# Hybrid attention block in split float32: the order of work in the gated stage and in front of the output projection

## Chip, cores and metric

One NeuronCore of a Trainium2 chip runs the whole kernel as one program. The metric is the device time of one execution in microseconds (us), lower is better. In the profile PE is TensorE's matmul, PEld its weight load, DVE VectorE, ACT ScalarE, POOL GpSimd, and SP SyncE, which here only issues DMAs.

## The reference

One decoder layer on x of 1024 tokens by 1024 channels, all in float32. What matters here is its end. `o_a` and `o_b` are the outputs of two attention mixers (512 channels each), `z_a`, `z_b`, `m_a`, `m_b` are parts of the input projection, and `gate` is the third part of a conditioning vector:

```
mod = c @ w_ada + b_ada                      # shift, scale, gate
y_a = (merge_heads(o_a) * silu(z_a)) @ w_o_nsa
y_b = (merge_heads(o_b) * silu(z_b)) @ w_o_swa
y = (sigmoid(m_a) * y_a + sigmoid(m_b) * y_b) @ w_out
x = x + gate[:, None, :] * rms_norm(y, g_post)
```

## The kernel before

Every float32 operand of a matmul is held as a high part (a copy rounded to the format of TensorE's fast float32) and a low part (operand minus high part), and every product is made of three matmuls: high by high, high by low, low by high. A matmul has 128 output rows and 512 columns. Splitting a weight tile is a cast (the high part) and a subtraction on GpSimd (the low part).

The first stages (conditioning, norm, projections, attention) are not touched. Near the end of attention, blocks of the input projection still run as filler behind a pace set by `hold`; it is cleared at L892. Then come two stages.

**The gated stage** (L896 to L982). `oh`, `ol` are the high and low parts of the eight head tiles, loaded from DRAM as `t1` tiles (named `od` in the code) and split: cast on ScalarE L909, subtraction on VectorE L910. Tiles 4 to 7 belong to side B, 0 to 3 to side A. The first two merge gates are made by projections (L918); the other fourteen are read back from DRAM into `t2` tiles (four buffers), and ScalarE applies the sigmoid (L916). `gated` (L929) then makes one block of 128 output rows: it loads one weight tile `w_o`, splits it (`split_half`: cast L151 on VectorE, subtraction L157 on GpSimd), and makes two halves of 512 columns, 12 matmuls each (L937 to L939). A loop over the eight blocks of side B writes the product with the gate to `ym` (L949, VectorE). A loop over the eight blocks of side A multiplies by the gate (L970, VectorE), adds to `ym` (L971, GpSimd), and splits the sum into `ymh` (L980, ScalarE) and `yml` (L981, VectorE). Behind each block of side A, `w_out_block` loads a row block of the last weight matrix in two halves and splits it: cast L962 on VectorE, subtraction L963 on GpSimd. These go to the places of the normalised input `hh`, `hl`, which the two projected gates read last. All raw weight tiles, `w_o` and `w_out`, share three buffers named `wraw`.

**The output projection** (L984 to L1033). The gate part of the conditioning is formed first: the eight row blocks of `w_adaT` in sixteen half-width loads into `t1` tiles, each reduced on VectorE against a broadcast of c (L992), then two products of `ones` with a diagonal tile `dg`, which lies in a `t2` buffer (L1001 on VectorE, L1004 on TensorE), then copies to `ggb` (L1005). For each of eight row tiles, two halves of 24 matmuls (L1017 to L1019) are followed by the sum of squares (L1021), scaling, adding x and the store.

The tile framework orders the instructions of each engine by the program order, by its own estimate of when operands are ready, and by the buffers. Each engine, and SyncE's queue of DMAs, then runs its list strictly in order.

## Time and profile before

| | us |
|---|---|
| median of three runs (940.97 to 942.63) | 942.55 |
| the profiled execution | 939.97 |
| its span | 938.1 |
| TensorE busy in the span | 913.6 |
| matmuls of the gated stage end (last one's start, rounded) | 833.9 |
| last matmul of the program starts | 931.15 |

The span runs from the first to the last instruction of the profiled execution, whose own time is 1.87 us more. A busy TensorE is not TensorE at its peak: matmuls are pipelined, and a row's duration (0.39) is longer than the distance to the next row (0.23).

### The profile page before, as it was taken

Reading aid. Unit: us, or ns where it says so; the run is one execution under the profiler, and the core shown is the slowest. Engines: PE = TensorE matmul, PEld = TensorE weight load, DVE = VectorE, ACT = ScalarE, POOL = GpSimd, SP = SyncE. Lnnn points to the kernel's source line nnn. Section 1 sums busy time; section 2 is a strip of 40 time slices with the busy share of each in tenths; the row PEclk is TensorE's granted clock in tenths of the full one; section 3 lists DMA queues with packets and bytes.
Section 4 is the critical chain, followed back from the end, with each engine's and each line's share of the span. In section 5 each row is a group of like instructions: output and inputs, shape, how many; then the busy total and the mean of one; then the engine's idle time right before and its main releaser. Section 6 shows DMA issues by size and latency. Waiting matters only on the chain.

```text
span 938.1 us, 14375 instructions
## 1 busy us (share of the span) xinstructions
PE 913.6 (97%) x4584; PEld 762.0 (81%) x4584; DVE 568.9 (61%) x1557; ACT 486.7 (52%) x1116; POOL 380.5 (41%) x438
## 2 busy tenths in 40 slices
PE   9979999999999999999999999999999999979997
PEld 8869888888888878868878888887887888858885
DVE  5847563376677776684676755565664379872322
ACT  5566632266776776584666765665554421342111
POOL 0001212256575874453533764543351226871000
PEclk9989999999999999999999999999999999989999
DMA  8960452323232321212101222111111679621232
GB/s 309 313 216 33 162 165 86 122 79 102 81 106 82 125 60 39 80 35 68 59 32 35 80 68 80 55 48 57 58 46 56 218 234 303 194 89 45 90 107 84
DMA packets 65166, 100.84 MB, mean 107 GB/s; under 512 B 7617, under 2 KB 24385, under 8 KB 65090
## 3 DMA queue, kind: packets, MB, share of 16 engines
q1 hardware_dynamic: 64082, 98.73, 32.4%
q10 hardware_dynamic: 1008, 1.19, 0.4%
q8 instruction: 36, 0.59, 0.2%
q14 instruction: 40, 0.33, 0.1%
HBM read 79.97 MB, written 19.92 MB: 106 GB/s over the span
## 4 chain that ended last, share of the span: by engine, by line
PE 49%; POOL 2%; DVE 2%; DMA 2%; issue 1%; ACT 1%; DVEq 0%; POOLq 0%; SPq 0%; ACTq 0%
PE b_pj L177 6%; PE b_pt L778 6%; PE b_pj L182 5%; PE b_pj L183 5%; PE b_pv L789 3%; PE b_s L725 3%; PE b_pv L786 3%; PE b_s L728 3%; DMA wraw<-in_w_out 1%; PE b_s L1018 1%; PE b_s L1017 1%; PE b_s L1019 1%; POOL ym L971 1%; POOL wol L963 1%; PE b_pj L1017 1%
## 5 line engine op out<-in xcount | busy, mean ns | idle before, releaser
L157 POOL TENSOR_TENSOR wl<-wraw,wh 128x512 fp32r<-128x512 f32 x102 | 134.1, 1315 | 248.3 <-DVE wh L151 145.8
L177 PE MATMUL b_pj<-hh,wh 128*128 128x512 f32 x528 | 210.2, 398 | 0.0
L183 PE MATMUL b_pj<-hh,wl 128*128 128x512 f32 x528 | 208.2, 394 | 0.0
L182 PE MATMUL b_pj<-hl,wh 128*128 128x512 f32 x528 | 207.7, 393 | 0.0
L785 DVE TENSOR_TENSOR pl<-b_pt,ph 128x512 fp32r<-128x512 f32 x178 | 120.7, 687 | 35.6 <-ACT ph L784 34.7
L784 ACT CAST ph<-b_pt 128x512 fp32r<-128x512 f32 x178 | 101.9, 584 | 64.5 <-PE b_pt L778 57.0
L183 PEld LDWEIGHTS b_pj<-hh,wl 128*128 128x128 f32 x528 | 99.3, 188 | 18.9
L177 PEld LDWEIGHTS b_pj<-hh,wh 128*128 128x128 f32 x528 | 99.4, 188 | 17.9
L182 PEld LDWEIGHTS b_pj<-hl,wh 128*128 128x128 f32 x528 | 99.4, 188 | 17.5
L725 PE MATMUL b_s<-kh,q 128*128 128x256 f32 (+6 forms) x264 | 86.6, 334 | 1.4 <-DVE rr L753 0.8
L749 ACT ACTIVATE ps<-ps,mins 128x256 f32<-128x256 f32 (+7 forms) x96 | 65.0, 679 | 38.4 <-DVE mins L735 36.7
L761 POOL TENSOR_SCALAR ps<-ps,rr,gates 128x128 f32<-128x128 f32 (+7 forms) x64 | 52.9, 832 | 78.8 <-DVE rr L753 68.8
L728 PE MATMUL b_s<-kl,q 128*128 128x256 f32 (+6 forms) x264 | 84.0, 323 | 0.0
L749 ACT ACTIVATE pw<-pw,mins 128x256 f32<-128x256 f32 (+4 forms) x96 | 60.6, 632 | 31.5 <-DVE mins L735 29.4
L789 PE MATMUL b_pv<-pl,V 128*128 128x512 f32 x162 | 69.9, 431 | 1.6 <-DVE pl L785 1.4
L786 PE MATMUL b_pv<-ph,V 128*128 128x512 f32 x162 | 68.0, 420 | 0.3 <-ACT ph L784 0.2
L761 POOL TENSOR_SCALAR pw<-pw,rr,gates 128x640 f32<-128x640 f32 (+4 forms) x64 | 47.4, 744 | 50.6 <-DVE rr L753 44.4
L154 ACT CAST wh<-wraw 128x512 fp32r<-128x512 f32 x74 | 45.5, 617 | 36.9 <-PE b_pj L182 35.2
L725 PEld LDWEIGHTS b_s<-kh,q 128*128 128x128 f32 x264 | 49.8, 189 | 10.0 <-DVE mins L735 1.9
L800 POOL TENSOR_TENSOR ot<-ot,zt 64x512 f32<-64x512 f32 x32 | 41.2, 1287 | 34.9 <-DVE ot L799 28.6
L728 PEld LDWEIGHTS b_s<-kl,q 128*128 128x128 f32 x264 | 49.8, 189 | 6.1
L778 PE MATMUL b_pt<-ident,ps 128*128 128x128 f32 x344 | 52.4, 273 | 0.0
(296 smaller groups left out, 1883.8 us busy)
## 6 DMA issues: line engine op xcount, KB each, us to landing
wraw<-in_w_blk SPq DMA_DIRECT2D x90, 256.0 KB, 2.8
wa<-in_w_adaT SPq DMA_DIRECT2D x16, 512.0 KB, 4.9
w1raw<-in_w SPq DMA_DIRECT2D x16, 256.0 KB, 3.4
od<-ot SPq DMA_DIRECT2D x64, 64.0 KB, 2.1
sp_MA<-sp SPq DMA_DIRECT2D x16, 256.0 KB, 2.0
wraw<-in_w_o SPq DMA_DIRECT2D x16, 256.0 KB, 3.8
t<-od SPq DMA_DIRECT2D x16, 256.0 KB, 3.4
xr<-in_x SPq DMA_DIRECT2D x16, 256.0 KB, 4.0
```

The source lines that it names most:

```text
L157: chain("wl", nc.gpsimd.tensor_tensor(wl, raw, wh.bitcast(F32), ALU.subtract))
L177: ins = nc.tensor.matmul(t, lhsT=wh, rhs=hh[kc][half], start=(kc == 0), stop=False)
L182: nc.tensor.matmul(t, lhsT=wh, rhs=hl[kc][half], start=False, stop=False)
L183: nc.tensor.matmul(t, lhsT=wl, rhs=hh[kc][half], start=False, stop=(kc == KC - 1))
L725: ins = nc.tensor.matmul(sp[:, :n_in], lhsT=q, rhs=rh, start=True, stop=False)
L728: nc.tensor.matmul(sp[:, :n_in], lhsT=q, rhs=rl, start=False, stop=True)
L749: nc.scalar.activation(rows[r][:, :off], rows[r][:, :off], AF.Exp, scale=-1.0, bias=mins[:, n - 1, r : r + 1], accum_out=sums[:, r : r + 1])
L761: nc.gpsimd.tensor_scalar(rows[r][:, :off], rows[r][:, :off], rr[:, r : r + 1], gate, ALU.mult, ALU.mult)
L778: ins = nc.tensor.transpose(t[:kw, r * P : r * P + P], rows[r][:, off : off + kw], ident)
L784: nc.scalar.copy(ph[:kw], t[:kw])
L785: nc.vector.tensor_tensor(pl[:kw], t[:kw], ph[:kw].bitcast(F32), ALU.subtract)
L789: nc.tensor.matmul(pv, lhsT=v, rhs=pl[:kw], start=False, stop=(last and n == len(todo) - 1))
```

## The change

Four edits, all behind the attention stage. (1) `ended` is set where `hold` is cleared; from then on `split_half` casts weights on ScalarE, not on VectorE, for the two projected gates and all of `w_o`. The cast of `w_out` moves to ScalarE too. (2) `w_out_block(m)` is called behind each block of side B, ahead of side A; head tiles 0 to 3 are loaded inside that loop, one behind every second block. (3) The sum of the sides is made on VectorE. (4) The gate part of the conditioning loads eight full-width tiles, into places that the gated stage leaves (`ym7`, `oh1`, `ol1`, ..., with c in `ym6`), and its two products stand behind the products of the first two row tiles, which are issued two ahead of their evaluation.

```
-        if low is None and hold[0] is None:
+        if low is None and hold[0] is None and not ended:
             ins = nc.vector.tensor_copy(wh, raw)
             after(ins, last["dve"])
         else:
...
     hold[0] = None
+    ended.append(True)
...
-        for k in (4, 5, 6, 7, 0, 1, 2, 3):
+        def heads_out(k):
             for half in range(2):
...
+        for k in range(4, 8):
+            heads_out(k)
...
-        for m in range(8):
-            ym[m] = op.tile([P, S], F32, name=f"ym{m}", tag=f"ym{m}")
-            gated(m, "B", 1, lambda sl, ty, sg: nc.vector.tensor_tensor(ym[m][:, sl], ty, sg, ALU.mult))
...
-                nc.vector.tensor_copy(a[n], raw)
+                nc.scalar.copy(a[n], raw)
                 nc.gpsimd.tensor_tensor(b[n], raw, a[n].bitcast(F32), ALU.subtract)
...
         for m in range(8):
+            ym[m] = op.tile([P, S], F32, name=f"ym{m}", tag=f"ym{m}")
+            gated(m, "B", 1, lambda sl, ty, sg: nc.vector.tensor_tensor(ym[m][:, sl], ty, sg, ALU.mult))
+            if m % 2:
+                heads_out(m // 2)
+            w_out_block(m)
+        for m in range(8):
             def emit(sl, ty, sg):
                 nc.vector.tensor_tensor(sg, ty, sg, ALU.mult)
-                nc.gpsimd.tensor_tensor(ym[m][:, sl], ym[m][:, sl], sg, ALU.add)
+                nc.vector.tensor_tensor(ym[m][:, sl], ym[m][:, sl], sg, ALU.add)
             gated(m, "A", 0, emit)
...
-            w_out_block(m)
...
-        cbs = [tmp("xr", 3), tmp("xr", 3)]
...
+        cb2 = op.tile([P, D], F32, name="cb2", tag="ym6")
+        nc.sync.dma_start(cb2, io["c"].partition_broadcast(P))
+        for k, place in enumerate(("ym7", "oh1", "ol1", "oh2", "ol2", "oh3", "ol3", "oh1")):
             blk = 16 + k
+            wa = op.tile([P, D], F32, name="wa", tag=place)
+            nc.sync.dma_start(wa, io["w_adaT"][blk * P : (blk + 1) * P, :])
+            nc.vector.tensor_tensor_reduce(
+                out=wa, in0=wa, in1=cb2, scale=1.0, scalar=smalls[:, 8 + blk : 9 + blk],
+                op0=ALU.mult, op1=ALU.add, accum_out=mod[:, blk : blk + 1])
...
+        ahead = [out_products(0), out_products(1)]
+        gate_rows()
+        for i in range(NT):
+            out_rows(i, ahead.pop(0))
+            if i + 2 < NT:
+                ahead.append(out_products(i + 2))
```

`out_products(i)` holds the 48 matmuls of a row tile, `out_rows(i, ts)` what follows them, and `gate_rows` the diagonal tiles, the two products with `ones` and the copies to `ggb`; their bodies are the lines that stood in the loop before.

TensorE's order at the end of the gated stage, before (`oh3`, `ol3` are a head tile's parts; L1004 is a product with `ones`, L1017 to L1019 are products of the first row tile):

```order
L939 MATMUL b_pv_9218<-oh3_8251,wl_9197 128x512
L1004 MATMUL b_pt_9308<-t2_9309,ones_75 128x512
L1017 MATMUL b_pj_9322<-woh0_8824,ymh0_8816 128x512
L1018 MATMUL b_pj_9322<-wol0_8825,ymh0_8816 128x512
L1019 MATMUL b_pj_9322<-woh0_8824,yml0_8817 128x512
```

and in the changed kernel (line numbers shifted; L944 is the last gated matmul, L1011 the product with `ones`):

```order
L944 MATMUL b_pv_9230<-oh3_8251,wl_9209 128x512
L1020 MATMUL b_pt_9282<-woh0_8463,ymh0_8912 128x512
L1021 MATMUL b_pt_9282<-wol0_8464,ymh0_8912 128x512
...
L1022 MATMUL b_s_9357<-woh7_8866,yml7_9249 128x512
L1011 MATMUL b_pt_9382<-t2_9383,ones_75 128x512
L1011 MATMUL b_pj_9387<-t2_9388,ones_75 128x512
L1020 MATMUL b_s_9413<-woh0_8463,ymh0_8912 128x512
```

The products with `ones` moved from directly behind the gated stage to behind 96 products; the first product that reads `yml7` stands 26 matmuls behind the gated stage.

VectorE's order at the end of side A in the changed kernel (L978 the product with the gate, L979 the sum of the sides, L989 the low part, ISA the reductions of the conditioning):

```order
L978 TENSOR_TENSOR t2_9243<-b_pv_9230,t2_9243 128x512
L989 TENSOR_TENSOR yml7_9249<-ym7_8809,ymh7_9248 128x512
L979 TENSOR_TENSOR ym7_8809<-ym7_8809,t2_9243 128x512
L997 ISA wa_9262,mod_83<-wa_9262,cb2_9254,smalls_79 128x1024
L997 ISA mod_83 128x1
L989 TENSOR_TENSOR yml7_9249<-ym7_8809,ymh7_9248 128x512
L997 ISA wa_9259,mod_83<-wa_9259,cb2_9254,smalls_79 128x1024
```

The sums joined VectorE's list between the gate products and the low parts, and all eight reductions now stand behind them, one of them ahead of the last low part.

SyncE's DMAs at the start of side B, before (`in_w_o` weights of a gated block, `od` head tiles, `in_w_out` the last matrix):

```order
L908 DMA t1_8300<-od0_118 128x512
L908 DMA t1_8304<-od1_119 128x512
L908 DMA t1_8308<-od1_119 128x512
L908 DMA t1_8312<-od2_120 128x512
L908 DMA t1_8316<-od2_120 128x512
L908 DMA t1_8320<-od3_121 128x512
L959 DMA wraw_8822<-in_w_out 128x512
L908 DMA t1_8324<-od3_121 128x512
L991 DMA t1_9258<-in_w_adaT 128x512
```

and in the changed kernel (L910 head tiles, L961 the last matrix, L145 weights of a gated block):

```order
L910 DMA t1_8292<-od7_125 128x512
L961 DMA wraw_8575<-in_w_out 128x512
L910 DMA t1_8508<-od0_118 128x512
L145 DMA wraw_8582<-in_w_o 128x512
L910 DMA t1_8512<-od0_118 128x512
L961 DMA wraw_8630<-in_w_out 128x512
L910 DMA t1_8622<-od1_119 128x512
L961 DMA wraw_8636<-in_w_out 128x512
L910 DMA t1_8626<-od1_119 128x512
L145 DMA wraw_8643<-in_w_o 128x512
```

Between two loads for gated blocks now stand two loads of the last matrix and three half head tiles, where before the head tiles stood in a row; the conditioning's loads are gone from here. The `in_w_o` load first shown is the tenth that takes a `wraw` buffer from the first gated block's on, for block 3 of side B; block 0 of side A has the twenty-fifth.

## Rows read from the trace of the kernel before

**Rows 1.** The first part of the profile's page: busy time of each engine, its share of the span and its number of instructions.

```profile
PE 913.6 (97%) x4584; PEld 762.0 (81%) x4584; DVE 568.9 (61%) x1557; ACT 486.7 (52%) x1116; POOL 380.5 (41%) x438
```

**Rows 2.** Busy time of each engine in six stretches (us from the span's start): stage of side B, stage of side A, the gap, the time right behind it, the output projection, the tail. Behind the engines stand the granted TensorE clock as a share of 2.4 GHz, the mean busy share of the DMA engines, and GB/s.

```profile
747.10:790.80 43.70, 43.70 (x194) 36.19 (x193) 34.58 (x63) 10.69 (x18) 18.66 (x13) 1.00 0.82 264
790.80:834.20 43.40, 43.40 (x193) 35.69 (x191) 36.98 (x47) 15.02 (x25) 36.58 (x25) 1.00 0.57 184
834.20:840.20 6.00, 0.15 (x2) 0.04 (x1) 3.30 (x6) 3.52 (x6) 2.97 (x2) 0.83 0.30 94
840.20:846.10 5.90, 5.90 (x12) 3.69 (x13) 3.60 (x6) 1.19 (x3) 3.90 (x3) 0.59 0.00 0
846.10:931.40 85.30, 85.30 (x377) 70.38 (x375) 23.40 (x46) 11.96 (x34) 4.49 (x8) 1.00 0.26 84
931.40:938.10 6.70, 0.14 (x1) 0.00 (x0) 2.22 (x4) 0.69 (x2) 0.55 (x1) 0.68 0.21 79
```

**Rows 3.** TensorE's instructions in order of time around the end of the gated stage, and its last one: start, duration (a matmul's end is modelled and overlaps the next), line, operation; in brackets the idle time before it and what ended that.

```profile
833.93 0.39 PE L939 MATMUL b_pv<-oh,wl 128*128 128x512 f32 x1
...
840.17 2.07 PE L1004 MATMUL b_pt<-t,ones 128*128 128x512 f32 x2 [5.84 <-DVE t L1001]
...
846.12 0.39 PE L1019 MATMUL b_pj<-woh,yml 128*128 128x512 f32 x1
...
849.77 0.39 PE L1017 MATMUL b_s<-woh,ymh 128*128 128x512 f32 x1
...
931.15 0.39 PE L1019 MATMUL b_s<-woh,yml 128*128 128x512 f32 x1
```

**Rows 4.** Who waited for whom around the gap (834 to 850 us): the waits of the compute engines, us in total, times, longest.

```profile
PE b_pt L1004 <- DVE t L1001: 5.8, 1, 5.8
...
DVE t L1001 <- POOL ym L971: 2.3, 2, 1.2
```

**Rows 5.** The same for the DMA queue that SyncE issues, over the gated stage (747 to 850 us).

```profile
SPq L915 <- POOL ym L971: 20.6, 12, 3.0
...
SPq L959 <- POOL wol L963: 7.8, 9, 1.3
...
SPq L144 <- POOL wl L157: 5.0, 5, 1.6
```

**Rows 6.** VectorE, GpSimd and ScalarE behind the end of the gated matmuls, in order of time (one row of each engine).

```profile
844.27 0.69 DVE L970 TENSOR_TENSOR t<-b_pv,t 128x512 f32<-128x512 f32 x1
...
843.84 1.65 POOL L971 TENSOR_TENSOR ym<-ym,t 128x512 f32<-128x512 f32 x1 [1.41 <-DVE t L970]
...
846.77 0.62 ACT L980 CAST ymh<-ym 128x512 fp32r<-128x512 f32 x1
```

**Rows 7.** Groups of instructions by line in the gated stage (747.1 to 834.2 us): busy us, mean ns of one, then the idle time before them and its releasers.

```profile
L963 POOL TENSOR_TENSOR wol<-wraw,woh 128x512 fp32r<-128x512 f32 x16 | 23.4, 1468 | 12.0 <-DVE woh L962 12.0
...
L971 POOL TENSOR_TENSOR ym<-ym,t 128x512 f32<-128x512 f32 x11 | 16.8, 1538 | 1.2 <-DVE t L970 1.2
...
L157 POOL TENSOR_TENSOR wl<-wraw,wh 128x512 fp32r<-128x512 f32 x11 | 15.5, 1409 | 18.4 <-DVE wh L151 14.4 <-DMA wraw<-in_w_out 2.9 <-DVE amod L996 1.0
...
L962 DVE CAST woh<-wraw 128x512 fp32r<-128x512 f32 x16 | 14.6, 916 | 2.3 <-DMA wraw<-in_w_out 2.3
...
L992 DVE CUSTOM_DVE_ANT_0 t<-t,xr,mod 128x512 f32<-128x512 f32 x8 | 9.6, 1201 | 0.9 <-DMA t<-in_w_adaT 0.8
...
L992 DVE CUSTOM_DVE_ANT_0 t<-t,xr,smalls 128x512 f32<-128x512 f32 x8 | 6.8, 846 | 1.5 <-DMA t<-in_w_adaT 1.5
...
L909 ACT CAST oh<-t 128x512 fp32r<-128x512 f32 x10 | 6.2, 622 | 9.8 <-DMA t<-od 9.7
...
L151 DVE CAST wh<-wraw 128x512 fp32r<-128x512 f32 x11 | 6.2, 564 | 2.2 <-DMA wraw<-in_w_o 1.6 <-PE b_s L939 0.6
```

**Rows 8.** Single lines: the low part of the merged rows on VectorE, and the reduction of the conditioning in the first stage at full width (duration ns min/median/max, first and last start).

```profile
L981 DVE TENSOR_TENSOR yml<-ym,ymh x16: 676/1114/1780, 806.4 to 847.4; 128x512 fp32r<-128x512 f32 x16
...
L265 DVE CUSTOM_DVE_ANT_0 wa<-wa,cb,smalls x16: 1278/1280/1284, 13.0 to 47.5; 128x1024 f32<-128x1024 f32 x16
```

**Rows 9.** The loads that share the three raw weight buffers, from the first load of the last matrix to its last (L959 that matrix, L144 the head-side weights): issues with first and last start, then the time to landing.

```profile
L959 SPq DMA_DIRECT2D wraw<-in_w_out x16: 327/328/398, 759.2 to 815.4; - x16
...
DMA to landing us min/median/max: 2.7/3.7/5.0
...
L144 SPq DMA_DIRECT2D wraw<-in_w_o x7: 328/328/383, 766.0 to 810.8; - x7
...
DMA to landing us min/median/max: 2.6/4.1/4.8
```

**Rows 10.** The first stage, where conditioning weights are loaded in pieces of 512 KB while nothing else is large: the stretch of 10 to 50 us (columns as in rows 2), and the time to landing of these loads.

```profile
10.00:50.00 40.00, 39.98 (x224) 35.89 (x223) 34.25 (x67) 21.55 (x40) 0.00 (x0) 1.00 0.89 307
...
DMA to landing us min/median/max: 3.6/4.7/9.5
```

**Rows 11.** The end of attention, around 720 us: a weight cast on VectorE, two rows of ScalarE, and TensorE's next wait.

```profile
720.23 0.42 DVE L151 CAST wh<-wraw 128x512 fp32r<-128x512 f32 x1
...
719.93 0.59 ACT L816 COPY sp<-b_pj 128x512 f32<-128x512 f32 x1 [0.34 <-PE b_pj L183]
...
720.83 0.59 ACT L784 CAST ph<-b_pt 128x512 fp32r<-128x512 f32 x1 [0.31 <-PE b_pt L778]
...
722.19 0.50 PE L789 MATMUL b_pv<-pl,V 128*128 128x512 f32 x1 [0.23 <-DVE pl L785]
```

More of the change, by code (lines that the diff above doesn't have):

```diff
@@ L93, in hybrid_kernel @@
     hold = [None]
+    ended = []
     done = [0.0]
@@ L981, in hybrid_kernel @@
                 nc.vector.tensor_tensor(yml[m][:, sl], ym[m][:, sl], ymh[m][:, sl].bitcast(F32), ALU.subtract)
-            w_out_block(m)
-        cbs = [tmp("xr", 3), tmp("xr", 3)]
-        for n in range(2):
-            nc.sync.dma_start(cbs[n], io["c"][n * HS : n * HS + HS].partition_broadcast(P))
-        for k in range(KC):
-            blk = 16 + k
-            for n in range(2):
-                wa = tmp("t1", 3)
-                nc.sync.dma_start(wa, io["w_adaT"][blk * P : (blk + 1) * P, n * HS : n * HS + HS])
-                nc.vector.tensor_tensor_reduce(
-                    out=wa, in0=wa, in1=cbs[n], scale=1.0,
-                    scalar=mod[:, blk : blk + 1] if n else smalls[:, 8 + blk : 9 + blk],
-                    op0=ALU.mult, op1=ALU.add, accum_out=mod[:, blk : blk + 1])
+        cb2 = op.tile([P, D], F32, name="cb2", tag="ym6")
@@ L996, in hybrid_kernel @@
         nc.vector.tensor_tensor(amod, mod[:, 16:24], g_post, ALU.mult)
         ggb = op.tile([P, D], F32, name="ggb")
-        for n in range(2):
-            t = anybank()
-            dg = tmp("t2", 4)
-            nc.vector.tensor_tensor(
-                dg.rearrange("p (k t) -> p k t", k=4), ident.unsqueeze(1).broadcast_to([P, 4, P]),
-                amod[:, 4 * n : 4 * n + 4].unsqueeze(2).broadcast_to([P, 4, P]), ALU.mult)
-            nc.tensor.matmul(t, lhsT=ones, rhs=dg, start=True, stop=True)
-            nc.scalar.copy(ggb[:, n * HS : n * HS + HS], t)
@@ L1006, in hybrid_kernel, with gate_rows @@
-        for i in range(NT):
+        def gate_rows():
+            for n in range(2):
+                t = anybank()
+                dg = tmp("t2", 4)
+                nc.vector.tensor_tensor(
+                    dg.rearrange("p (k t) -> p k t", k=4), ident.unsqueeze(1).broadcast_to([P, 4, P]),
+                    amod[:, 4 * n : 4 * n + 4].unsqueeze(2).broadcast_to([P, 4, P]), ALU.mult)
+                nc.tensor.matmul(t, lhsT=ones, rhs=dg, start=True, stop=True)
+                nc.scalar.copy(ggb[:, n * HS : n * HS + HS], t)
@@ L1007, in hybrid_kernel, with out_products @@
+        def out_products(i):
             sl = slice(i * P, i * P + P)
-            xr = tmp("xr", 3)
-            xs = [xr, tmp("xr", 3)]
-            ss = sm.tile([P, 2], F32, name="ss", tag="ss", bufs=2)
-            yg = []
+            ts = []
             for n in range(2):
-                ns = slice(n * HS, n * HS + HS)
-                nc.sync.dma_start(xs[n], io["x"][sl, ns])
                 t = anybank()
@@ L1019, in hybrid_kernel, with out_rows @@
                     nc.tensor.matmul(t, lhsT=yml[k][:, sl], rhs=woh[k][n], start=False, stop=(k == 7))
+                ts.append(t)
+            return ts
+        def out_rows(i, ts):
+            sl = slice(i * P, i * P + P)
+            xs, yg = [], []
+            ss = sm.tile([P, 2], F32, name="ss", tag="ss", bufs=2)
+            for n, t in enumerate(ts):
+                ns = slice(n * HS, n * HS + HS)
+                xs.append(tmp("xr", 3))
+                nc.sync.dma_start(xs[n], io["x"][sl, ns])
                 jk = tmp("t2", 4)
@@ L1028, in hybrid_kernel @@
             nc.gpsimd.tensor_tensor(rs, rs, neg1, ALU.pow)
-            nc.vector.tensor_tensor(yg[1], t, ggb[:, HS:], ALU.mult)
+            nc.vector.tensor_tensor(yg[1], ts[1], ggb[:, HS:], ALU.mult)
             for n in range(2):
```

## The prediction

> **What bounds the kernel now.** I read the page first: TensorE is busy 97% of the span [rows 1], so only its idle or slow time can be won. The table by stretches says where that is [rows 2]: in both sides of the gated stage TensorE is full at a granted clock of 1.00, in the output projection again; between them lie 6.0 us without work and 5.9 us at a mean clock of 0.59, that is mostly at the lower of its two levels (1.2 of 2.4 GHz), behind that idle time. TensorE's own rows give the size [rows 3]: the last gated matmul starts at 833.93, the next instruction comes 5.84 us late and is the product with `ones` for the conditioning, and full pace (0.227 us per matmul) is back at 846.12.
>
> The waits name the cause: TensorE waits for VectorE's diagonal tile, which waits for a sum of the sides on GpSimd [rows 4], since that sum frees the `t2` buffer. The second thing to see is that this is not the only late work. VectorE forms the last gate product at 844.27, GpSimd's last sum starts at 843.84, and a cast of `ymh` still starts at 846.77 [rows 6]: the chain behind the matmuls is some 10 us late. It is late because GpSimd is busy 36.58 of 43.40 us in side A [rows 2], with eleven sums and the splits of both weights [rows 7], and because the loads of the gates wait 20.6 us for the sums [rows 5]. Taking away only the product with `ones` would put the wait on `yml7`.
>
> **The gap, the main term.** From 834.16 (833.93 plus one distance of 0.227) to 931.38 are 97.22 us. The work in it is 384 products (8 row tiles, 2 halves, 24 each) and two products with `ones`. Between 849.77 and 931.15 lie 359 distances [rows 3], so one is 81.38 / 359 = 0.2267 us; 384 of them are 87.05. A product with `ones` is two float32 rows: at the low clock the pair took 2.07 [rows 3], at the full clock I take half of that less a little latency, 0.87; two are 1.74. So 88.8 us are needed and 97.22 - 88.8 = 8.4 us are to be had, if nothing is late next and the clock stays at 1.00.
>
> **Is anything late next?** First the chain to `yml7`. Its last gate product can start when the stage ends; the sum of that half belongs to later row tiles. For the first half, a low part follows on VectorE at 0.68 each, the shortest of its line [rows 8], so it is ready 1.5 us behind the stage; the order has 26 matmuls first, 5.9 us. Cover 4.4 us. In side A VectorE now has 48 such instructions (16 gate products, 16 sums, 16 low parts), 48 x 0.68 = 32.6 of 43.4 us, since the casts and, in side B, the reductions are gone from it (16.4 us of L992, 14.6 of L962, 6.2 of L151 [rows 7]). GpSimd loses its sums (1.54 us each [rows 7]) and gains nothing.
>
> A low part took up to 1.78 us, with a median of 1.11, against 0.68 at best [rows 8], beside a GpSimd that hardly paused. The Trainium skill, SBUF — State Buffer, section on who interferes with whom, says that a VectorE instruction with two SBUF inputs and a GpSimd instruction that reads SBUF lock each other out for a whole instruction; that speaks against the sums on VectorE, which have two such inputs. By that rule the eight weight splits left on GpSimd in side A, 1.41 us each, add at most 11.3 us to the 32.6, 43.9 against 43.4: half a microsecond, inside the cover. By the rows' median for the 32 instructions with two inputs the load would be 46.6, 3.2 us too much, inside the cover too.
>
> Second the conditioning. Its eight loads of 512 KB and the broadcast of c, 4.72 MB, can be issued from some 833 us, when the last side A half leaves `oh1`. In the first stage such loads ran at 307 GB/s [rows 10]: 15.4 us. Then the last reduction, 1.28 [rows 8], and a diagonal tile, 0.7: ready at about 852. A slower bound: the first stage's sixteen reductions came one in 2.16 us (13.0 to 47.5 [rows 8]) with other loads between; 833 + 4.7 to the first landing [rows 10] + 8 x 2.16 + 2 gives 857. TensorE needs it behind 96 products, at 834.2 + 21.8 = 856.0. I take no wait, and 1 to 2 us as the far end, on the loads' own rate, as nothing else moves much then.
>
> **Side B, the price.** What was a dense stage gets 16 loads of the last matrix, their casts and their splits. ScalarE: 25.7 us busy in both sides [rows 2] plus 36 casts of 0.62, as the cast L909 takes [rows 7], make 48 of 87.1. GpSimd in side B: 24 splits of 1.47 make 35 of 43.7. Both fit. The tight place is the three `wraw` buffers. From the tenth load (issued at about 749, by the time of the same head tiles now) to the twenty-fifth, which block 0 of side A needs, are 15 loads. That block starts at 747.1 + 8 x 24 x 0.2267 = 790.6; with 4.1 us landing [rows 9], a cast of 0.62, a split of 1.29 and 0.4 of signals its load must be issued by 784.2. So a load may take 35.2 / 15 = 2.35 us. Before, 23 loads went from 759.2 to 815.4 [rows 9], 2.55 each, which would make TensorE wait 3 us. A turn of a buffer by its parts (4.1 landing, 0.62, 1.29) is 6.0 us, 2.0 per load. I take the parts: the old pace was not the buffers' own, since the queue stood 20.6 us for sums that leave GpSimd and 12.8 us for splits [rows 5], and a cast of `w_out` took 0.92 us beside GpSimd on VectorE [rows 7]. Cost nothing, far end 3 us.
>
> **The end of attention.** Six weight casts now stand on ScalarE between the casts of the probabilities. Around 720 us a cast of 0.6 comes beside a copy at 719.93 and pushes the cast at 720.83; TensorE then already waits 0.23 us [rows 11]. It costs between 0 and 1.2 us (two such places); I take 0.3, since elsewhere ScalarE pauses and VectorE is relieved.
>
> **Sum.** 8.4 - 0.3 = 8.1 us. The profiled execution goes from 939.97 to 931.9, its span from 938.1 to 930.0. It is 2.6 us below the median of the three runs; the middle of these four executions is 941.8, and 941.8 - 8.1 = **933.7 us**. About 0.2% (1.9 us) can be told from no change.
>
> **Rivals.**
> - *The buffers are slow* (chance 0.12): the old pace of 2.55 us per load stays, TensorE waits 3 us before side A: 936.7. For it: the observed pace. Against: what set that pace leaves.
> - *The buffers stall the stage, slower than before* (0.06): the loads of the last matrix hold `wraw` while loads of head tiles stand ahead of them in the same queue. A wait of over 2.35 us x 15 loads and a slow clock behind it, priced at 2.4 us (5.9 us in which 3.5 us of work were done [rows 2, 3]), cancel the gain and more from 2.85 us per load. At 3.1 us TensorE waits 11.3: 933.7 + 13.7 = 947. For it: three buffers, landings up to 5.0 us [rows 9]. Against: it needs a turn of over 8.5 us where the parts make 6.0.
> - *The conditioning is late* (0.06): 1 to 2 us of wait behind 96 products, 935.5.
> - *VectorE becomes the bound in side A* (0.05), so that the change does not take the chain off the path: at 1.3 us, between the median and the longest of the low parts [rows 8], the 32 instructions and 16 gate products make 52.5, 9.1 us late, 4.4 of it covered, 4.7 of the gain gone, 938.4. For it: GpSimd still reads the same memory. Against: it has eight instructions left there.
> - *The casts on ScalarE lie on the path* (0.04): 36 x (0.62 - 0.42) = 7.2 us of the gain go, 940.9. For it: 0.62 against 0.42 [rows 7, 11]. Against: ScalarE is idle for half of the stage. The Trainium skill, ScalarE: Activation LUTs, rules for kernel authors, sends simple elementwise work to VectorE as the faster engine; by that rule the casts moved the wrong way.
>
> **How the numbers follow.** The forecast keeps 0.67. The low end, 930.5, is the gain of 8.4 without the 0.3 against the profiled execution's own time (931.6), less 1 us for the spread of runs. The high end, 940.0, takes in the slow buffers, the late conditioning and the VectorE case; outside lie the casts on the path and the stall. Faster by over 0.2%: the forecast, the slow buffers, the late conditioning and VectorE make 0.90, less 0.03 for a VectorE worse than priced, 0.87; within 0.2%: these 0.03 and the casts, 0.07; slower: the stall, 0.06.
>
> **What would show it.** Right: no row of TensorE idle by over 1 us between 747 and 931, granted clock 1.00 throughout; the sums at 0.7 us on VectorE; the last gate product within 1 us of the last gated matmul; the products with `ones` behind 96 products without a wait; loads of `wraw` at about 2.0 us each in side B. Wrong: an idle row before a gated block that ends with GpSimd's split of a weight (buffers), one before the product with `ones` that ends with VectorE (conditioning), or one at `yml7`.

## The result, and the profile after

| | before | after |
|---|---|---|
| median of five runs each, us | 942.36 (940.70 to 942.63) | 932.66 (931.76 to 932.78) |
| ratio, 95% interval | | 0.9906 (0.9894 to 0.9918) |
| the profiled execution, its span | 939.97, 938.1 | 932.78, 931.0 |
| first gated matmul to the end of the last product | 184.26 | 175.85 |

The change is faster by 9.7 us in the medians, by 7.1 in the spans of the two profiles, and by 8.4 in the stretch that it touches. The last figure is the one to keep. The ratio stands for 8.9 us, and where the kernel before was run again beside the experiments (11 to 22 runs each time) its median was 941.3 to 941.5, against which 932.66 is a gain of 8.6 to 8.9. The 8.4 us are measured from the first gated matmul (747.12 before, 748.76 after) to one distance of 0.23 behind the last product, a stretch that I call **the stage** below. Up to the end of attention the code ahead of it is the same, and the profile after came 1.64 us late to it; 1.31 of it are there at the end of a wait in the first stage, whose row was 56.25 with 6.27 us of idle time in the profile before:

```profile
57.56 1.39 PE L200 MATMUL b_s<-wvh,hh 128*128 128x408 f32 x3 [6.88 <-ACT hh L296]
```

Over the profiles of this study, all with this code, that wait took 6.2 to 7.6 us, which is why the experiments are read by their stages first.

The profile after, to be held against [rows 1, 2]: the page's line of engines, then stretches for side B, side A, what follows up to the last product, and the tail (columns as in [rows 2]).

```profile
PE 909.4 (98%) x4584; PEld 760.2 (82%) x4584; DVE 549.2 (59%) x1521; ACT 506.7 (54%) x1152; POOL 354.9 (38%) x422
```

```profile
748.76:792.30 43.54, 43.54 (x194) 36.06 (x193) 22.69 (x27) 25.54 (x42) 31.98 (x23) 1.00 0.79 246
792.30:835.80 43.50, 43.50 (x194) 36.02 (x192) 28.39 (x43) 19.69 (x34) 5.24 (x4) 1.00 0.36 113
835.80:924.60 88.80, 88.80 (x389) 72.64 (x387) 37.40 (x71) 13.34 (x35) 3.85 (x7) 1.00 0.40 133
924.60:931.00 6.40, 0.17 (x1) 0.00 (x0) 2.23 (x4) 0.69 (x2) 0.55 (x1) 0.85 0.21 82
```

TensorE is full and at a granted clock of 1.00 from the first gated matmul to the last product; the stretches of 6.0 us idle and 5.9 us at a clock of 0.59 are gone. Its own rows, to be held against [rows 3]: the last gated matmul, the first product that reads the last low part, the products with `ones`, and the last product. None has idle time before it.

```profile
835.57 0.39 PE L944 MATMUL b_pv<-oh,wl 128*128 128x512 f32 x1
...
841.69 0.39 PE L1022 MATMUL b_pt<-woh,yml 128*128 128x512 f32 x1
...
857.56 1.02 PE L1011 MATMUL b_pt<-t,ones 128*128 128x512 f32 x2
858.41 1.02 PE L1011 MATMUL b_pj<-t,ones 128*128 128x512 f32 x2
...
924.38 0.39 PE L1022 MATMUL b_s<-woh,yml 128*128 128x512 f32 x1
```

The chain behind the gated matmuls, to be held against [rows 6], on VectorE:

```profile
837.82 0.68 DVE L978 TENSOR_TENSOR t<-b_pv,t 128x512 f32<-128x512 f32 x1
838.65 0.69 DVE L989 TENSOR_TENSOR yml<-ym,ymh 128x512 fp32r<-128x512 f32 x1
839.26 0.69 DVE L979 TENSOR_TENSOR ym<-ym,t 128x512 f32<-128x512 f32 x1
841.81 1.28 DVE L997 CUSTOM_DVE_ANT_0 wa<-wa,cb,smalls 128x1024 f32<-128x1024 f32 x1 [1.87 <-DMA cb<-in_c]
...
853.42 1.29 DVE L1008 TENSOR_TENSOR t<-ident,amod 128x512 f32<-128x512 f32 x2
```

The last gate product starts at 837.82, where it started at 844.27. The two diagonal tiles are done at 854.7, and the products with `ones` come at 857.56.

**Lateness.** For the experiments I need one more number, worked out from rows. The gated stage has 32 halves of 12 matmuls, 2.72 us each in a dense stage. The lateness of half n is the start of its gate product on VectorE less (first gated matmul + n x 2.72). For the last half after: 837.82 - (748.76 + 87.05) = 2.0. The table gives it for the first half of side A (17) and the last (32), with all idle time of TensorE in the stage. The edits are numbered as in the change. Each ratio is taken against runs of the kernel before that were measured beside that kernel, so ratios and stages compare better than medians.

| kernel | edits in it | median, us | ratio to before (95%) | late, half 17 | late, half 32 | idle | stage |
|---|---|---|---|---|---|---|---|
| before | none | 942.36 | | 6.5 | 10.1 | 5.84 | 184.26 |
| e1_order | order of 4 only | 942.49 | 1.0006 (0.9994, 1.0018) | 7.8 | 10.7 | 6.84 | 186.17 |
| e6_sums_only | 3 | 942.95 | 1.0017 (1.0006, 1.0027) | 5.6 | 10.6 | 6.02 | 184.37 |
| e8_edit4_only | 4 | 941.47 | 0.9998 (0.9988, 1.0009) | 8.6 | 9.9 | 5.99 | 184.77 |
| e7_wout_only | 2 | 937.67 | 0.9954 (0.9938, 0.9969) | 10.1 | 8.0 | 2.81 | 180.41 |
| e11_edits14 | 1, 4 | 938.88 | 0.9977 (0.9967, 0.9987) | 0.3 | 7.3 | 3.73 | 181.75 |
| e13_edits24 | 2, 4 | 932.57 | 0.9908 (0.9889, 0.9927) | 2.9 | 0.2 | 0 | 175.85 |
| e2_no_edit4 | 1, 2, 3 | 937.48 | 0.9953 (0.9935, 0.9970) | 10.7 | 9.1 | 3.73 | 181.62 |
| e4_wout_sideA | 1, 3, 4, head tiles of 2 | 939.11 | 0.9977 (0.9966, 0.9988) | 0.7 | 8.2 | 3.60 | 182.69 |
| e3_sums_pool | 1, 2, 4 | 932.40 | 0.9902 (0.9887, 0.9917) | 2.2 | 0.2 | 0 | 175.85 |
| e5_casts_dve | 2, 3, 4 | 932.17 | 0.9911 (0.9893, 0.9929) | 3.9 | 3.6 | 0 | 175.85 |
| after | all | 932.66 | 0.9906 (0.9894, 0.9918) | 1.6 | 2.0 | 0 | 175.85 |
| e9_extra_dve | all, VectorE loaded | 937.57 | 0.9954 (0.9938, 0.9971) | 9.7 | 8.2 | 3.55 | 181.70 |
| e10_extra_loads | all, queue loaded | 934.32 | 0.9923 (0.9908, 0.9937) | 3.1 | 2.4 | 0.91 | 177.35 |

Where the last half is late by 3.6 us or less, TensorE never waits behind the stage; where by 7.3 or more, it does. A longer stage is more than its idle time, since slower matmuls follow the waits: with edit 4 alone the granted clock is 0.62 from 842.99 to 852.00. In two kernels, the ones with edit 2 alone and with more loads, weights come late as well; there TensorE itself falls behind the dense stage, by 3.3 and 1.5 us, and the lateness holds that too.

### The profile page after: what moved, and what is told of

Read it like the earlier page. It is cut to its first block, busy times and chain, and to the rows that moved or that the text cites. A ratio compares the mean times of both kernels' runs of the same rounds, so it can differ in the third digit from the quotient of the medians.

```text
span 931.0 us, 14317 instructions
## 1 busy us (share of the span) xinstructions
PE 909.4 (98%) x4584; PEld 760.2 (82%) x4584; DVE 549.2 (59%) x1521; ACT 506.7 (54%) x1152; POOL 354.9 (38%) x422
## 4 chain that ended last, share of the span: by engine, by line
PE 54%; ACT 1%; DVE 1%; issue 0%; DMA 0%; POOL 0%; DVEq 0%; POOLq 0%; ACTq 0%
PE b_pj L178 5%; PE b_pj L183 5%; PE b_pj L184 5%; PE b_pt L779 5%; PE b_pv L790 3%; PE b_s L726 3%; PE b_s L729 3%; PE b_pv L787 3%; PE b_s L1022 1%; PE b_s L1021 1%; PE b_s L1020 1%; PE b_s L943 1%; PE b_s L942 1%; PE b_s L944 1%; PE b_pt L1021 1%; PE b_pj L943 1%
## 5 line engine op out<-in xcount | busy, mean ns | idle before, releaser
L155 ACT CAST wh<-wraw 128x512 fp32r<-128x512 f32 x94 | 57.9, 618 | 46.9 <-PE b_pj L183 39.9
```

## Experiments: one edit alone

**The order of the products with `ones` alone.** In the kernel before, only the tail of the program is that of the change:

```
+        ahead = [out_products(0), out_products(1)]
+        gate_rows()
         for i in range(NT):
+            out_rows(i, ahead.pop(0))
...
```

> The kernel before with one half of edit 4 alone: the products with ones stand behind 96 products, everything else (conditioning loads, sums on GpSimd, last matrix in side A, casts on VectorE) stays. Measure: from the first gated matmul to the last product of the program, 184.3 us in the profile before, 175.9 in that of the change. My theory: the chain of sums, casts and low parts is late by itself, so TensorE goes on for some 26 products and then waits at the low part of row block 7 (or one before it); ready at about 844 on the scale of before against 840.1 needed: about 4 us idle and 2.4 us of slow clock. Stage 182 us (180 to 184), time about 940 (938.5 to 942). Rival, the product with ones was the whole trouble: no wait, stage 176, time about 934.

Measured: no gain, and the stage 1.9 us longer. TensorE's rows with idle time behind the gated stage:

```profile
842.13 0.50 PE L1016 MATMUL b_pt<-woh,ymh 128*128 128x512 f32 x1 [2.42 <-ACT ymh L980]
843.25 0.79 PE L1018 MATMUL b_pt<-woh,yml 128*128 128x512 f32 x1 [0.39 <-DVE yml L981]
848.07 0.80 PE L1016 MATMUL b_pt<-woh,ymh 128*128 128x512 f32 x1 [4.03 <-ACT ymh L980]
```

The wait went from the products with `ones` to the high and low parts of the last row blocks: 6.84 us instead of 5.84. So the product with `ones` was only the first to meet a chain that is late as a whole, as the prediction said.

**The sums on VectorE alone.**

```
-                nc.gpsimd.tensor_tensor(ym[m][:, sl], ym[m][:, sl], sg, ALU.add)
+                nc.vector.tensor_tensor(ym[m][:, sl], ym[m][:, sl], sg, ALU.add)
```

> The kernel before with edit 3 alone: the sums of the sides on VectorE. Theory that GpSimd's queue is the cause: the sums follow the gate products at 0.7 us, the diagonal tiles find their t2 buffers free, the product with ones comes within 2 us of the stage's end although VectorE in side A has 37.0 + 16 x 0.68 = 47.9 us of work in 43.4; stage 178 us (176 to 181), time about 936. Rival, two-input instructions on VectorE are slowed by GpSimd beside them and VectorE's list becomes the late one: low parts and sums of 1.1 us in the mean, VectorE some 15 us late, idle of 5 us or more stays; stage 183 to 186, time 941 to 944.

Measured: no gain; if anything slower by 0.2%. The stretch of side A (columns as in [rows 2]), and then TensorE's wait for the product with `ones`:

```profile
791.70:835.20 43.50, 43.50 (x193) 35.85 (x191) 37.13 (x56) 14.60 (x25) 19.83 (x14) 1.00 0.55 180
```

```profile
PE b_pt L1004 <- DVE t L1001: 6.0, 1, 6.0
```

GpSimd fell from 36.58 to 19.83 us, and the wait stayed at 6.0. The rival's number came true, but not its reason: the sums took 0.68 us in the median and 0.82 in the mean, against 0.78 in the mean in the change, and not 1.1. Taking the sums from GpSimd is not enough. This run alone does not clear GpSimd, since VectorE took on what GpSimd lost; the kernels without edit 4 and without edit 2 do: their chains are 9 and 8 us late at the end with GpSimd busy only 10.14 and 16.51 us in side A. **A chain this late needs no loaded GpSimd.** A row of before hinted at it: GpSimd's last sum had 1.41 us of idle time before it that ended with VectorE's gate product [rows 6].

**Edit 4 alone**, conditioning and order:

```
+        for k, place in enumerate(("ym7", "oh1", "ol1", "oh2", "ol2", "oh3", "ol3", "oh1")):
...
+            wa = op.tile([P, D], F32, name="wa", tag=place)
...
+        ahead = [out_products(0), out_products(1)]
+        gate_rows()
```

> The kernel before with the whole of edit 4 alone: conditioning loaded behind the gated stage in full tiles, products with ones behind 96 products. New theory: what makes VectorE late are the conditioning's loads and reductions among the gates of side B; how late a gate product starts behind its last matmul (6.5 us for the first of side A in the profile before, 10.1 for the last, 1.6 and 2.0 in that of the change) falls to about 3 at the start of side A. In side A the sums stay on GpSimd behind the splits of the last matrix, so it grows again, to 6 to 8, and TensorE waits 2 to 5 us at a low part, then runs on the slow clock. Stage 181 us (178 to 184), time 939. Rival, the theory of the prediction (GpSimd's load alone makes it late): the last gate product 10 us late as before, stage 184 to 187, time 942 to 943.

Measured: nothing gained. The side-B stretch, what VectorE waited for from 760 to 834 us, and four rows of its list:

```profile
748.70:792.30 43.60, 43.60 (x194) 36.09 (x194) 22.26 (x39) 11.23 (x18) 19.69 (x15) 1.00 0.62 195
```

```profile
DVE woh L962 <- DMA wraw<-in_w_out: 27.0, 14, 3.7
```

```profile
786.40 0.43 DVE L962 CAST woh<-wraw 128x512 fp32r<-128x512 f32 x1 [2.99 <-DMA wraw<-in_w_out]
788.08 0.43 DVE L962 CAST woh<-wraw 128x512 fp32r<-128x512 f32 x1 [1.25 <-DMA wraw<-in_w_out]
788.42 0.42 DVE L151 CAST wh<-wraw 128x512 fp32r<-128x512 f32 x1
788.75 0.68 DVE L949 TENSOR_TENSOR ym<-b_s,t 128x512 f32<-128x512 f32 x1
```

VectorE is only half busy in side B, and its products still go from 1.7 us late (half 7) to 10.8 (half 16). The casts of the last matrix, which the framework moved up into side B, stand in its list ahead of the gate products, and each waits up to 3.7 us for its load (12.7 us of the 27.0 fall in side B). The last row is the product of half 12, 7.4 us late behind two such casts. The lateness of 3 us that I expected at the start of side A came out at 8.6 for that reason.

**Edit 2 alone**, the last matrix in side B:

```
+            if m % 2:
+                heads_out(m // 2)
+            w_out_block(m)
         for m in range(8):
...
-            w_out_block(m)
```

> The kernel before with edit 2 alone: the last weight matrix loaded and split in side B, its casts still on VectorE, the sums still on GpSimd. Theory of GpSimd's queue: in side A it now has 16 sums and 8 splits, 24.6 + 11.3 = 36 us in 43.4, where before 59 us were wanted; the sums come within 2 us of the gate products, the product with ones without a wait. VectorE in side B has 34.6 + 14.6 = 49 us in 43.7, and catches up in side A. Stage 177 us (175.8 to 180), time about 935. Rival, the splits beside a full VectorE stall the weights of side B (TensorE waits for a weight's low part before some gated block): stage 181 or more, time 939 or more.

Measured: 4 us gained, half of it all. Both expectations hold a part. Behind the stage almost no wait is left (0.34 and 0.33 us), but TensorE waits for weights around the end of side B (0.47, 0.68 and 0.99 us), and the last gated matmul comes 90.15 us behind the first where 86.8 are dense.

## Experiments: one edit left out of the change

**Without edit 4.** Conditioning and products with `ones` as before, the rest as in the change:

```
-        cb2 = op.tile([P, D], F32, name="cb2", tag="ym6")
...
+        cbs = [tmp("xr", 3), tmp("xr", 3)]
...
+            for n in range(2):
+                wa = tmp("t1", 3)
```

> The changed kernel without edit 4: conditioning in half tiles and the products with ones directly behind the gated stage, as before; casts on ScalarE, last matrix in side B and sums on VectorE stay. Theory: once GpSimd's sums are gone the diagonal tiles have their buffers at the end of the stage, so the order of the products with ones costs nothing: no idle over 1 us, stage 176 us (175.8 to 178), time 932.7 (within 0.2% of the change). Rival, the cover of 96 products is what wins: the product with ones waits 3 us or more for VectorE and the clock falls behind it, stage 180 or more, time 937 or more.

Measured: 4.8 us of the gain are gone.

```profile
838.57 2.07 PE L1011 MATMUL b_pt<-t,ones 128*128 128x512 f32 x2 [3.73 <-DVE t L1008]
```

The rival's size is right and its reason is half of it. The gate products enter side A 10.7 us late, against 1.6 in the change, though sums and casts are away from GpSimd and VectorE. What differs in side B is the conditioning. Three things come with it, which this run does not tell apart: 19.8 us of reductions on VectorE, 7.6 us that they wait for their loads, and 8.6 us that SyncE's queue stands for them (747 to 805 us). (The other mixture, the conditioning behind the stage and the products with `ones` directly there too, was not tried. The rows of the change speak against it: the diagonal tiles are done at 854.7 there, 19 us behind the gated matmuls, so the order of the products goes with that place of the conditioning.)

**Without edit 3**, the sums back on GpSimd (the one line of the experiment above, reversed).

> The changed kernel with edit 3 undone: the sums back on GpSimd, which has only eight splits beside them in side A. New theory: a gate tile, its sigmoid, the cast of the merged rows and the low part form a ring with the sum, two halves a turn; with sums on VectorE a turn took 5.0 to 5.2 us against 5.44 of TensorE. On GpSimd (1.54 instead of 0.68 us, one more handover) it takes 6.0, so the lateness grows by 0.3 us per half, from 2 to about 6.5 us; TensorE waits 2 to 4 us at row block 7 and has a slow clock behind it: stage 180 us (177 to 183), time 937. Rival, the lateness comes from side B alone and the engine of the sums does not matter: stage 176, time 932.7.

Measured: the same time as the change; the last gate product comes 0.2 us late instead of 2.0. My expectation of a lateness that grows fell. I take it that leaving the sum out of VectorE's list made room there for what it cost on GpSimd; no run shows that by itself.

**Without edit 2 for the last matrix** (the head tiles stay where edit 2 put them).

```
             if m % 2:
                 heads_out(m // 2)
-            w_out_block(m)
...
                 nc.vector.tensor_tensor(yml[m][:, sl], ym[m][:, sl], ymh[m][:, sl].bitcast(F32), ALU.subtract)
+            w_out_block(m)
```

> The changed kernel with edit 2 undone for the last matrix: its loads, casts (on ScalarE) and splits stand in side A again, one block behind each gated block. Theory of the in-order list: a cast that waits for its load holds back what stands behind it on its engine. In side A ScalarE's list has the gates' sigmoids and the casts of the merged rows behind these casts, so the gate products grow late from under 2 us to 6 us or more, TensorE waits 2 to 4 us at row block 7 with a slow clock behind it: stage 180 us (177 to 183), time 937. Rival, ScalarE has room (30 of 43 us busy) and waits for gate loads anyway: stage 176, time 932.7.

Measured: 6.5 us of the gain are gone. Side B is in time to its end (0.3 us late), and then one half of side A loses ten. First VectorE, then ScalarE at that place:

```profile
795.10 1.36 DVE L978 TENSOR_TENSOR ym<-ym,t 128x512 f32<-128x512 f32 x1
805.83 1.37 DVE L988 TENSOR_TENSOR yml<-ym,ymh 128x512 fp32r<-128x512 f32 x1 [9.37 <-ACT ymh L987]
```

```profile
796.99 0.63 ACT L921 ACTIVATE t<-t 128x512 f32<-128x512 f32 x1 [2.65 <-DMA t<-sp_MA]
797.83 0.62 ACT L964 CAST woh<-wraw 128x512 fp32r<-128x512 f32 x1 [0.21 <-DMA wraw<-in_w_out]
798.81 0.62 ACT L964 CAST woh<-wraw 128x512 fp32r<-128x512 f32 x1 [0.36 <-DMA wraw<-in_w_out]
...
803.17 0.63 ACT L921 ACTIVATE t<-t 128x512 f32<-128x512 f32 x1 [2.66 <-DMA t<-sp_MA]
804.66 0.62 ACT L964 CAST woh<-wraw 128x512 fp32r<-128x512 f32 x1 [0.86 <-DMA wraw<-in_w_out]
805.18 0.62 ACT L987 CAST ymh<-ym 128x512 fp32r<-128x512 f32 x1
```

The sum is there at 796.5; its cast `ymh` could start then and starts at 805.18, behind seven casts and sigmoids, five of which wait for a load. VectorE, with nothing wrong of its own, stands 9.37 us for it. It is not the casts' loads alone: from 787 to 835 us ScalarE's sigmoids wait 15.8 us for gate loads and its casts 5.5 us for the last matrix. Both kinds of load stand in one queue. The load of the gate whose sigmoid starts at 803.17 was issued at 800.23, right behind a load of a weight at 799.85 that had waited for a raw buffer, which a split on GpSimd freed.

**Without edit 1**, the casts on VectorE:

```
-        if low is None and hold[0] is None and not ended:
+        if low is None and hold[0] is None:
...
-                nc.scalar.copy(a[n], raw)
+                nc.vector.tensor_copy(a[n], raw)
```

> The changed kernel with edit 1 undone: the casts of all weights on VectorE again, among them those of the last matrix, which stand in side B. Theory of the in-order list: these casts wait for their loads (27 us of waits on VectorE with edit 4 alone) and hold the gate products behind them; products start side A 5 us late or more and stay so, TensorE waits 2 to 4 us at row block 7 with a slow clock behind it: stage 180 us (178 to 183), time 937. Rival, VectorE without the conditioning has room (16.4 us went, 24 casts of 0.42 to 0.92 come): stage 176, time 932.7.

Measured: the same time as the change, so the rival holds. The products are up to 10.3 us late in side B (half 12), but back at 3.9 when side A begins.

## Experiments: the cause by itself, and the smallest change

**Load on VectorE, and load in the queue.** The change, with one of these behind each block of side B:

```
+            for _ in range(3):
+                nc.vector.tensor_tensor(scr, ym[m][:, :HS], ym[m][:, HS:], ALU.mult)
```

```
+            for n in range(2):
+                scr = tmp("xr", 3)
+                nc.sync.dma_start(scr, io["w_adaT"][(16 + m) * P : (17 + m) * P, n * HS : n * HS + HS])
```

> The changed kernel with 24 more instructions on VectorE in side B, three behind each block, 0.68 us each (products of finished rows into a tile that nothing reads): 16.4 us, as much as the conditioning's reductions had there before, and no loads. Theory that VectorE's load is what made the gate products late in side B: they start side A 6 us late or more, the last one 6 to 9 us late, TensorE waits at row block 7 for 3 us or more: stage 181 (179 to 184), time 938. Rival, the loads in SyncE's queue did it: the gate products start side A less than 4 us late, stage 176, time 932.7.

> The changed kernel with 16 more loads of 256 KB in side B, two for each block, into three buffers that nothing reads: what the conditioning had in SyncE's queue before, without its reductions. Theory that the loads in the queue delay the gate tiles: gate products start side A 5 us late or more; if so TensorE waits at row block 7, stage 179 or more, time 936 or more. Rival, only VectorE's load counts: less than 4 us late, stage 176 (up to 177), time 932.7 to 933.5.

Measured: the load on VectorE alone brings the lateness back (9.7 and 8.2 us) and 4.9 us of the time. It is a heavier load than I meant: the 24 instructions took 1.18 us in the median, 28.8 us together and not 16.4, against 19.8 us of reductions in the kernel without edit 4. So work on VectorE is shown to be enough by itself, but not that the reductions' work was enough without their waits. VectorE is busy 39.70 us of 43.50 in side B, so it fits by the sum and is still late:

```profile
749.90:793.40 43.50, 43.50 (x193) 36.04 (x192) 39.70 (x39) 23.02 (x38) 30.33 (x21) 1.00 0.70 223
```

```profile
841.97 0.50 PE L1027 MATMUL b_pt<-woh,ymh 128*128 128x512 f32 x1 [0.77 <-ACT ymh L995]
845.98 0.79 PE L1027 MATMUL b_pt<-woh,ymh 128*128 128x512 f32 x1 [2.78 <-ACT ymh L995]
```

The loads alone leave the gate products in time (3.1 and 2.4 us); they go into buffers that nothing reads, so the queue never stands for a reduction here. They cost 1.5 us in another place: a weight of side B comes late.

```profile
783.01 0.50 PE L942 MATMUL b_pt<-oh,wh 128*128 128x512 f32 x1 [0.74 <-ACT wh L155]
784.38 0.50 PE L944 MATMUL b_pt<-oh,wl 128*128 128x512 f32 x1 [0.17 <-POOL wl L158]
```

That is close to the rival that I called slow buffers: from the tenth to the twenty-fifth the loads of `wraw` come at 36.47 / 15 = 2.43 us each, more than the 2.35 that were allowed, and those of the last matrix take 5.1 us to landing in the median against 3.3 in the change. The loads of weights have little to spare.

**Edits 1 and 4.** To edit 4 alone, as shown above, only the casts on ScalarE are added.

> The kernel before with edits 1 and 4: casts on ScalarE, conditioning behind the stage; the last matrix stays in side A and the sums on GpSimd. Theory of the in-order list: VectorE's list has neither reductions nor waiting casts, so the products enter side A under 3 us late; in side A GpSimd has 24 splits and 16 sums, 59 us of work in 43, so the sums and with them the gates grow late to 6 to 10 us: TensorE waits 3 to 6 us at a low part, stage 182 us (179 to 186), time 939. Rival, taking VectorE's list clear is enough whatever GpSimd has: stage 176 to 177, time 933.

Measured: stage 181.75, as expected, and the products enter side A in time. But the waits point past GpSimd, which is busy 31.73 of 43.50 us in side A and not 59. Low parts waited 23.2 us for the cast `ymh` on ScalarE, 8.6 at once, and from 787 us on ScalarE's sigmoids waited 18.1 us for gate loads and its casts of the last matrix 3.7 us (14.0 from the start of side B): the picture of the experiment without edit 2.

**Edits 2 and 4.** The change, with edits 1 and 3 both reversed as shown above.

> The kernel before with edits 2 and 4 alone: last matrix in side B, conditioning behind the stage; the casts stay on VectorE and the sums on GpSimd. Theory after the runs so far: edits 2 and 4 are what wins, together, and edits 1 and 3 move work between engines that have room; gate products enter side A 4 to 6 us late and the last one is under 5 us late, no idle row of TensorE over 1 us from the first gated matmul on; stage 175.9 us (to 176.5), time within 0.2% of the change (931 to 934.5). Rival, edits 1 and 3 stand in for each other (each alone could be left out, but not both): the sum on GpSimd adds to the lateness of 3.6 us that the casts on VectorE gave, TensorE waits 1 to 3 us at row block 7 with a slow clock behind it: stage 178 to 181, time 935 to 938.

Measured: the whole gain, with the casts on VectorE and the sums on GpSimd. The stretches of sides B and A:

```profile
747.58:791.10 43.52, 43.52 (x193) 36.05 (x192) 29.32 (x46) 11.24 (x18) 28.88 (x23) 1.00 0.76 238
791.10:834.60 43.50, 43.50 (x193) 36.05 (x192) 25.72 (x37) 18.25 (x32) 27.64 (x20) 1.00 0.38 121
```

In side A GpSimd makes the sums (27.64 us busy), and the last gate product is 0.2 us late. **Edits 2 and 4 together make the whole gain; edits 1 and 3 neither help nor hurt in their company.** No kernel here beats the change: all four with a stage of 175.85 are one result.

## Why the prediction was right, and where it was not

**The main term** was exact, and the time came out at 932.66 for a forecast of 933.7. Of the 97.22 us from the last gated matmul to the end of the last product, 88.8 were said to be needed; after, they are 924.38 + 0.23 - 835.80 = 88.81. The stage lost 8.41 us, against 8.4.

**The cause of the lateness failed.** The prediction said that the chain is late because GpSimd is busy in side A, with the sums and the splits of both weights. Taking the sums from GpSimd alone changed nothing, and leaving them there, in the smallest version, lost nothing. And without edit 2 for the last matrix the chain is 8.2 us late at the end with no sum on GpSimd, which is busy only 16.51 of 43.56 us in side A. What the runs showed in its place has two parts. The chain is made late by what stands in the in-order lists of VectorE and ScalarE between its own steps: the conditioning in side B (leaving edit 4 out; the load on VectorE alone does the same), and the casts of the last matrix, with the loads that they and the gates wait for (in side A without edit 2 and with edits 1 and 4, from side B on with edit 4 alone). In the kernel before both were mostly work, 16.4 us of reductions and 14.6 of casts, and the casts waited only 2.3 us for loads [rows 7]; it is with the conditioning gone that their waits show. Two things stay open: how much of the conditioning's harm is VectorE's work and how much its loads' waits, and which step of load, cast, split and freed raw buffer sets the pace of the waiting casts. The second part is that in side A the chain recovers slowly. A turn of the chain in the change, mid side A, on VectorE and ScalarE:

```profile
811.25 0.69 DVE L979 TENSOR_TENSOR ym<-ym,t 128x512 f32<-128x512 f32 x1
...
814.52 0.63 ACT L921 ACTIVATE t<-t 128x512 f32<-128x512 f32 x1 [0.68 <-DMA t<-sp_MA]
...
815.19 0.62 ACT L988 CAST ymh<-ym 128x512 fp32r<-128x512 f32 x1
815.85 0.69 DVE L989 TENSOR_TENSOR yml<-ym,ymh 128x512 fp32r<-128x512 f32 x1
816.46 0.69 DVE L979 TENSOR_TENSOR ym<-ym,t 128x512 f32<-128x512 f32 x1
```

A sum frees a gate buffer, the next gate is loaded, its sigmoid runs, behind it the cast of the merged rows, then the low part and the next sum but one: 816.46 - 811.25 = 5.21 us for two halves, in which TensorE takes 5.44. That gives back 0.12 us per half. Without edit 4 the lateness falls from 10.7 to 9.1 over 15 halves, 0.11 each. That the turn sets this pace I read from the rows; no run took it apart, and it is not the same everywhere: with edit 4 alone the lateness falls from 15.5 (half 20) to 9.9 (half 32), 0.47 each, and in the kernel without edit 1 it falls by 6.4 us from half 12 to half 17. The loads' wait for sums, which the prediction took as a mark of trouble (20.6 us [rows 5]), is even longer after (747 to 850 us), and harmless:

```profile
SPq L920 <- DVE ym L979: 29.1, 12, 5.3
```

The number came out because the size was read from TensorE's gap, whatever made it. That the change as a whole removed the real cause along with the supposed one was luck: of the two edits meant for GpSimd's list, the sums turned out to be worth nothing, and the last matrix helped for another reason.

**The chain to `yml7`**: the last gate product was to come within 1 us of the last gated matmul and came 2.0 us behind it (837.82 against 835.80), behind earlier halves in VectorE's list. The low part that the first row tiles read, that of the half before, was done at 839.34, and the product that reads it comes at 841.69: a margin of 2.35 us, not 4.4. VectorE's 32.6 us in side A were 28.39, but only 43 instructions fall in that window where 48 were counted.

**The lock between VectorE and GpSimd.** The low parts and sums of the change, and VectorE's low parts of the head tiles (durations in ns, min/median/max):

```profile
L989 DVE TENSOR_TENSOR yml<-ym,ymh x16: 687/691/695, 801.3 to 843.0; 128x512 fp32r<-128x512 f32 x16
```

```profile
L979 DVE TENSOR_TENSOR ym<-ym,t x16: 682/684/1794, 797.3 to 839.3; 128x512 f32<-128x512 f32 x16
```

```profile
L912 DVE TENSOR_TENSOR ol<-t,oh x16: 692/1215/1770, 739.4 to 769.5; 128x512 fp32r<-128x512 f32 x16
```

In side A GpSimd is busy 5.24 us, and the low parts all run at 0.69; one of the sums took 1.79. The low parts of the head tiles, which have splits beside them, take 1.2 in the median. With the sums back on GpSimd (24.60 of 43.50 us busy) the median of the low parts of the merged rows is 1.108 again, but with edits 2 and 4 alone, where GpSimd is busy 27.64, it is 0.692, with a mean of 0.88 and single ones up to 1.55. The rule of the Trainium skill, SBUF — State Buffer, section on who interferes with whom, that a VectorE instruction with two SBUF inputs and a GpSimd instruction that reads SBUF keep each other waiting, agrees with these rows as far as they go: some are slowed beside a busy GpSimd, and none of the low parts beside an almost idle one. How much it costs is not read from GpSimd's busy share, and no run isolates what it did to the time.

**Side B**: loads of `wraw` were to come at 2.0 us each; from the tenth (752.10) to the twenty-fifth (780.98) they came at 28.88 / 15 = 1.93, and no weight was late. ScalarE's 48 us were 45.2 (25.54 + 19.69), GpSimd's 35 in side B were 31.98. The rivals of slow and stalling buffers did not come.

**The conditioning** was done at 854.7, 853.1 on the clock of before, between the 852 taken and the far end of 857. (The terms given for the first add up to 833 + 15.4 + 1.28 + 0.7 = 850.4, not 852; for the second, sixteen reductions have fifteen distances between them, which makes 2.30 us each and 858.) A wait of 1.87 for the broadcast of c is in it. The products with `ones` came at 857.56 without a wait.

**The end of attention** was priced at 0.3 us and cost nothing: the same three idle rows of 0.22 to 0.23 stand there as before [rows 11], and from 75.59 (77.28 after) to the first gated matmul both profiles take 671.5 us. The tail became 0.3 us shorter, 6.72 to 6.39, which the sum did not have. With these two, 8.7 us is what the profiles show for the change. The medians say 9.7 with an interval of 7.7 to 10.0. Against the later medians of the kernel before, 941.3 to 941.5, the gain is 8.6 to 8.9, so about a microsecond of the 9.7 belongs to the five runs of before.

**The casts on ScalarE**: leaving edit 1 out gave 932.17 against 932.66, no difference. The row of the Trainium skill, ScalarE: Activation LUTs, rules for kernel authors, that sends `relu`, `max`, `min`, `add` and `mul` to VectorE does not name a cast, which the prediction took in with them; a single cast is indeed shorter there (0.42 against 0.62 us), and the time of this kernel does not show it.

## What to carry to other kernels

A late chain is read where its lateness begins, not where it is first waited for: take its lateness against the bound engine at several places, and look in each engine's in-order list for what stands between its steps, above all instructions that wait for loads. Idle time before a suspect's own row speaks for it (GpSimd waited for VectorE before its last sum), and a low busy share clears nobody whose list can stand waiting (with edit 4 alone VectorE was half idle in side B and its products ten us late). When several edits win together, leave out one at a time: here two of four are the gain, and each of these two brings half of it or nothing alone.

## What was not expected of the hardware

A cast of 128x512 that is ready to run costs 0.62 us on ScalarE and 0.42 on VectorE here, but with its load still on the way it held VectorE's list for up to 3.7 us. And VectorE's low part of a tile takes 0.69 us beside an idle GpSimd, but beside a busy one no single figure holds: its median in side A was 1.11 us in the kernel before, 1.108 with only the sums back on GpSimd, and 0.692 with edits 2 and 4 alone, with GpSimd busy 36.58 of 43.40, 24.60 of 43.50 and 27.64 of 43.50 us.
